# A decoder layer in fp32 pairs: tokens loaded channels-first, RMS norm moved behind the projections

## The chip, the cores and the metric

The kernel runs on one core of one Trainium2 chip. The metric is the device time of one execution in microseconds (us); the profile's clock starts at the first instruction, and its span is a little shorter than the device time.

## What is computed

One layer for 512 tokens of 1024 channels, all in fp32. Cut to what matters here:

```python
def rmsnorm(x, g):
    y = x * lax.rsqrt(jnp.mean(x * x, axis=-1, keepdims=True) + EPS)
    return y * g

h = rmsnorm(x, g_mix)
z = h @ w_in                       # 1024 -> 9728 columns
rq, rk, rv, rg, aq, ak, av, gl = jnp.split(z, IN_OFFSETS, axis=-1)
# retention on rq, rk, rv with swish gate rg: ret_branch
# QK-norm and rotary on aq, ak; three attention groups with av: att_branch
gate_r, gate_a = jnp.split(jax.nn.sigmoid(gl + b_gate), 2, axis=-1)
x = x + (gate_r * ret_branch + gate_a * att_branch) @ w_o
x = x + jnp.square(jax.nn.relu(rmsnorm(x, g_mlp) @ w_up)) @ w_down
gate_p = jax.nn.sigmoid(rmsnorm(x, g_ple) @ w_ple_gate)
return x + gate_p * (p_i @ w_ple_proj)       # p_i: 512 x 256 embeddings
```

The factor 1/rms is one number for each token, so `(x * r * g) @ w` equals `r * ((x * g) @ w)`.

## The kernel before

Every matrix is held as a pair: a high part (`whi`, `hh`), rounded to the matmul's format by ScalarE, and a low part (`wlo`, `hl`), the rest, by VectorE. A product is three matmuls (`mm3`): high by high, high by low, low by high. The weights come in units of 512 KB; `plan` lists them in order of use. `fetch` loads a unit into one of 6 buffers (`raw`), `ahead` and `split_unit` turn it into the pair (4 buffers each). A unit of `w_in` is split with the gain `g_mix` on its rows (lines 226 to 229): one instruction of 128x512 on each engine for each 128 input channels, two for a unit of rows, four of 128x256 for a unit of the gates. A unit of another weight is split in one instruction of 128x1024, or in halves of 128x512 while `self.pinned` is set.

The projections put channels on the partitions as the contraction. `rows_gemm` makes token tiles (128 tokens by 512 columns) in four PSUM banks (`pg`); a bank is used again when `consume` has taken the one before out of it. `cols_gemm` makes channel tiles by 512 tokens (gates, MLP).

The order of work on each engine is that of the program text; Tile puts in the semaphores, and nothing overtakes on an engine. Deferred work (transposes, attention scores) stands in `self.queue` and is put in by `tick`, once every two k steps or so; a lag counts ticks.

The start goes as follows. `setup` queues all loads on SyncE (SP), at most eight in flight. The embeddings `p` come with tokens on the partitions, are transposed on TensorE (`pp`) and multiplied with `w_ple_proj` (`embed`: two halves of four token tiles, stored by `store` to DRAM for the end of the kernel). `norm_T` makes a token tile's sum of squares, 1/rms (`rstd`: VectorE `v`, GpSimd `r`) and `y = x * r`, then `split_T` transposes it on TensorE (`pt`) and writes the pair `hT`. Tiles 0 and 1 are normed inside `embed`, tiles 2 and 3 inside the first projection, the queries of attention group 0, which is written as a wave (`wave=norm`): unit m and token tile m come in together. Two small transposes (`turn`) bring the gain vectors onto the partitions.

Then come, in order: queries, keys and values of group 0, the same of groups 1 and 2, retention, the gates with the two output projections (`mix`), and the tail (`w_o`, MLP, the embeddings' gate). For each token tile of a query or key projection (`att_proj`, `consume`) ScalarE copies the bank to `zn` and squares it by heads, VectorE and GpSimd make the norm (`v`, `r`), VectorE multiplies, and `rotate` applies the rotary tables `C` and `S` (GpSimd one product, VectorE two and a sum, all named `ro`). `tables` builds `C` and `S` on GpSimd out of loaded constants (`rotc`, and the gains in `mg`). Twelve ticks later `heads_T` transposes the four tiles by heads (`ph`).

Of the kernel before, what the change touches and what calls it, by code (L numbers as in the profile page):

```python
# [75 lines left out]
class Block:  # L76
# [63 lines left out]
    def evac(self, out, in_):  # L140
        self.ev ^= 1
        if self.ev:
            self.nc.scalar.activation(out, in_, AF.Copy)
        else:
            self.nc.vector.tensor_copy(out, in_)
# [256 lines left out]
    def setup(self):  # L402
        nc, a = self.nc, self.a
        rows = self.const.tile([48, P], F32, name="rows")
        names = ("g_mix", "ret_gn", "g_mlp", "g_ple", "b_gate")

        def row_loads(ns):
            for n in ns:
                o, k = 8 * names.index(n), a[n].shape[1] // P
                nc.sync.dma_start(rows[o : o + k], a[n][0].rearrange("(k p) -> k p", p=P))  # L410

        self.p_raw = self.wraw.tile([P, 1024], F32, tag="raw", name="p_raw").rearrange("p (t e) -> p t e", t=NT)
        nc.sync.dma_start(self.p_raw, a["p"][0, 0].rearrange("(t p) e -> p t e", p=P))
        self.fetch(1)
        row_loads(names[:1])
# [18 lines left out]
        self.gcol = self.const.tile([P, 48], F32, name="gcol")  # L434

        def turn(lo, hi):
            ps = self.bank()
            nc.tensor.transpose(ps[:, lo:hi], rows[lo:hi], self.ident[lo:hi, lo:hi])
            nc.vector.tensor_copy(self.gcol[:, lo:hi], ps[:, lo:hi])

        self.turn_mix = lambda: turn(0, 8)
        row_loads(names[1:])
        self.turn_rows = lambda: turn(0, 48)

# [22 lines left out]
    def embed(self, norm):  # L467
        nc = self.nc
        self.pinned = True
        pT = self.big("pT")  # L470
        hi, lo = pT[:, 0:2], pT[:, 2:4]
        for g in range(2):
            ps = self.bank("pp")
            for t in range(2):
                for k in range(2):
                    nc.tensor.transpose(ps[:, (2 * k + t) * P : (2 * k + t + 1) * P],
                                        self.p_raw[:, 2 * g + t, k * P : (k + 1) * P], self.ident)
            pv = ps.rearrange("p (k t) -> p k t", k=2)
            o = slice(2 * g * P, 2 * (g + 1) * P)
            self.pin(nc.scalar.activation(R(hi[:, :, o]), pv, AF.Copy))  # L480
            nc.vector.tensor_tensor(R(lo[:, :, o]), pv, hi[:, :, o], op=ALU.subtract)
        self.turn_mix()
        self.pp_dram = self.dram.tile([S, D], F32, name="pp_dram", tag="pp_dram")
        for half in range(2):
            def store(t, ps):
                o = self.tmp("pp")
                self.evac(o, ps)
                nc.sync.dma_start(self.pp_dram[t * P : (t + 1) * P, 512 * half : 512 * (half + 1)], o)

            self.ahead(1)  # L490
            norm(half)
            if half == 0:
                self.ahead(2)
            else:
                self.force(("h", 0, 1))
# [47 lines left out]
    def att_proj(self, g, n, **kw):  # L543
# [4 lines left out]
        def consume(t, ps):  # L548
# [3 lines left out]
            nc.scalar.activation(zn, ps, AF.Copy)  # L552
# [510 lines left out]
```

## Time and profile before

| | |
|---|---|
| median of 3 runs | 1037.51 us (1036.36 to 1038.64) |
| profiled execution | 1038.66 us |
| its span | 1036.7 us, granted clock 0.996 |
| TensorE matmul busy | 1014.2 us (98%), 4810 instructions |
| VectorE busy | 676.6 us (65%) |
| ScalarE busy | 480.4 us (46%) |
| GpSimd busy | 137.8 us (13%) |
| moved by DMA | 128.81 MB, 124 GB/s in the mean |

A matmul is shown until its result has left the array, so a 128x512 matmul shows about 0.39 us while the next one starts 0.23 us after it. How fast TensorE goes is read from the starts. In rows of the timeline an engine comes after the start and the duration; "x2" joins neighbours of one kind; brackets tell how long the engine had been idle and who ended it. In rows of stretches each engine has its busy time and number of instructions, and the DMA's share and rate stand at the end.

### The profile page before, as it was taken

What the parts mean: (1) busy time and instruction counts of PE and PEld (TensorE: products, weight loads), DVE (VectorE), ACT (ScalarE), POOL (GpSimd) and SP (SyncE); (2) the same over time, 40 slices, a digit from 0 to 9 for tenths busy, and PEclk for the clock granted to TensorE, in tenths of its full rate; (3) what the DMA queues carried; (4) which work ended last, traced back from release to release, by engine and by line L of the source; (5) the groups of instructions that cost most, each with busy time, mean ns of one, the idle gap of its engine ahead of it and who ended that gap; (6) DMA issues with size and microseconds to landing.
All of it is one profiled execution on the core that took longest, in us unless ns stands there. A gap on an engine that the chain in (4) does not pass through costs nothing.

```text
span 1036.7 us, 12913 instructions
## 1 busy us (share of the span) xinstructions
PE 1014.2 (98%) x4810; PEld 848.4 (82%) x4810; DVE 676.6 (65%) x1017; ACT 480.4 (46%) x1012; POOL 137.8 (13%) x126
## 2 busy tenths in 40 slices
PE   8998989999999999999999999999999999999998
PEld 6776878988987788888888888988888888888877
DVE  5588766767686743545343344679769877867983
ACT  6534635465452442535342323665455355355461
POOL 0264043123025501000010000000000000000000
PEclk9999999999999999999999999999999999999999
DMA  9532312323321222222323422354753753845711
GB/s 330 180 116 69 99 42 63 101 62 102 102 69 54 82 82 81 82 82 68 96 89 115 162 85 78 103 183 161 233 175 124 241 166 120 265 160 184 243 63 59
DMA packets 84766, 128.81 MB, mean 124 GB/s; under 512 B 6576, under 2 KB 39392, under 8 KB 84704
## 3 DMA queue, kind: packets, MB, share of 16 engines
q1 hardware_dynamic: 84704, 128.00, 38.7%
q8 instruction: 37, 0.61, 0.2%
q14 instruction: 25, 0.20, 0.1%
HBM read 123.77 MB, written 4.21 MB: 123 GB/s over the span
## 4 chain that ended last, share of the span: by engine, by line
PE 81%; DVE 8%; issue 2%; POOL 2%; ACT 1%; DMA 0%; DVEq 0%; ACTq 0%; POOLq 0%
PE pg L256 23%; PE pg L258 23%; PE pg L257 23%; DVE ro L510 2%; PE pb L256 2%; PE pb L258 2%; PE pb L257 2%; DVE wlo L224 1%; PE ph L522 1%; DVE wlo L229 1%; PE pt L365 1%; POOL r L355 1%; PE po L638 1%; PE sc L615 1%; DVE ro L512 1%
## 5 line engine op out<-in xcount | busy, mean ns | idle before, releaser
L256 PE MATMUL pg<-whi,hh 128*128 128x512 f32 x480 | 201.7, 421 | 1.6 <-ACT zn L552 0.8
L257 PE MATMUL pg<-wlo,hh 128*128 128x512 f32 x480 | 189.7, 395 | 2.1 <-DVE wlo L229 2.1
L258 PE MATMUL pg<-whi,hl 128*128 128x512 f32 x480 | 189.5, 395 | 0.0
L223 ACT ACTIVATE whi<-raw 128x1024 fp32r<-128x1024 f32 (+1 forms) x120 | 123.6, 1043 | 131.9 <-PE pg L257 39.0
L224 DVE TENSOR_TENSOR wlo<-raw,whi 128x1024 fp32r<-128x1024 f32 (+1 forms) x120 | 146.2, 1230 | 36.8 <-ACT whi L223 35.7
L229 DVE SCALAR_TENSOR_TENSOR wlo<-raw,gcol,whi 128x512 fp32r<-128x512 f32 (+1 forms) x184 | 122.2, 704 | 64.1 <-ACT whi L228 63.9
L228 ACT ACTIVATE whi<-raw,gcol 128x512 fp32r<-128x512 f32 (+1 forms) x184 | 107.4, 639 | 86.3 <-PE pg L258 53.1
L355 POOL TENSOR_TENSOR r<-v,mhalf 128x1 f32<-128x1 f32 (+1 forms) x52 | 40.5, 778 | 653.0 <-DVE v L354 653.0
L257 PEld LDWEIGHTS pg<-wlo,hh 128*128 128x128 f32 x480 | 99.3, 207 | 18.2 <-DVE wlo L229 4.6
L258 PEld LDWEIGHTS pg<-whi,hl 128*128 128x128 f32 x480 | 98.6, 205 | 17.4 <-DVE hl L379 0.4
L256 PEld LDWEIGHTS pg<-whi,hh 128*128 128x128 f32 x480 | 98.9, 206 | 16.2 <-ACT whi L228 1.2
L256 PE MATMUL pg<-h2h,whi 128*128 128x512 f32 (+1 forms) x288 | 105.5, 367 | 0.0
L257 PE MATMUL pg<-h2l,whi 128*128 128x512 f32 (+1 forms) x288 | 105.3, 366 | 0.0
L258 PE MATMUL pg<-h2h,wlo 128*128 128x512 f32 (+1 forms) x288 | 105.2, 366 | 0.0
L258 PEld LDWEIGHTS pg<-h2h,wlo 128*128 128x128 f32 x288 | 54.3, 189 | 8.8
L257 PEld LDWEIGHTS pg<-h2l,whi 128*128 128x128 f32 x288 | 54.3, 189 | 8.6
L256 PEld LDWEIGHTS pg<-h2h,whi 128*128 128x128 f32 x288 | 54.2, 189 | 8.7
L256 PE MATMUL pg<-hh,whi 128*128 128x512 f32 x128 | 52.4, 410 | 0.0
L257 PE MATMUL pg<-wlo,uh 128*128 128x512 f32 x128 | 50.1, 391 | 0.0
L258 PE MATMUL pg<-hh,wlo 128*128 128x512 f32 x128 | 50.0, 391 | 0.0
L257 PE MATMUL pg<-hl,whi 128*128 128x512 f32 x128 | 49.9, 390 | 0.0
L258 PE MATMUL pg<-whi,ul 128*128 128x512 f32 x128 | 49.9, 390 | 0.0
(176 smaller groups left out, 1838.4 us busy)
## 6 DMA issues: line engine op xcount, KB each, us to landing
raw<-in_w_down SPq DMA_DIRECT2D x80, 512.0 KB, 3.4
raw<-in_w_in SPq DMA_DIRECT2D x76, 512.0 KB, 3.8
raw<-in_w_up SPq DMA_DIRECT2D x32, 512.0 KB, 4.6
raw<-in_w_ret_out SPq DMA_DIRECT2D x8, 512.0 KB, 3.4
raw<-in_w_o SPq DMA_DIRECT2D x8, 512.0 KB, 3.5
raw<-in_w_ple_gate SPq DMA_DIRECT2D x8, 512.0 KB, 4.8
x<-in_x SPq DMA_DIRECT2D x8, 256.0 KB, 6.1
pp_dram<-pp SPq DMA_DIRECT2D x8, 256.0 KB, 4.1
```

The source lines that it names most:

```text
L223: self.pin(nc.scalar.activation(R(hi[:, i]), raw[:, i], AF.Copy))
L224: nc.vector.tensor_tensor(R(lo[:, i]), raw[:, i], hi[:, i], op=ALU.subtract)
L228: self.pin(nc.scalar.activation(R(hi[:, i]), raw[:, i], AF.Copy, scale=g))
L229: nc.vector.scalar_tensor_tensor(R(lo[:, i]), raw[:, i], g, hi[:, i], op0=ALU.mult, op1=ALU.subtract)
L256: t.matmul(ps, sh, mh, start=first, stop=False, skip_group_check=more)
L257: t.matmul(ps, sh, ml, start=False, stop=False, skip_group_check=more)
L258: t.matmul(ps, sl, mh, start=False, stop=last, skip_group_check=more)
L355: self.nc.gpsimd.tensor_tensor(r, v, self.mhalf[:, :w], op=ALU.pow)
L365: nc.tensor.transpose(ps[:, k * P : (k + 1) * P], part[:, k * P : (k + 1) * P], self.ident)
L510: nc.vector.tensor_tensor(v4(t2)[:, :, o0 : o0 + 64], v4(zn)[:, :, i0 : i0 + 64], bc(Sn[:, o0 : o0 + 64], 64), op=ALU.mult)
L512: nc.vector.tensor_tensor(o, t1, t2, op=ALU.add)
L522: self.nc.tensor.transpose(ps[:, t * P : (t + 1) * P], rots[t][:, h * HD : (h + 1) * HD], self.ident)
```

## The change

The host now hands over x, p and the gain vectors a second time, transposed (`x_cols`, `p_cols`, `vec_cols`); x is loaded in both forms. `embed` splits the transposed p, then multiplies x by g_mix channel by channel and splits that into `hT`, with no norm and no transpose. The first units of `w_in` are split in between, without gain. `token_factors` makes 1/rms of all 512 tokens from the other copy of x, and sends it through DRAM once to get it in the strided token order (`r_perm`). The queries of group 0 are no longer a wave. Where a projection leaves PSUM the token's factor is applied: as the scale of a copy (`zn`, `rz`, `v`), of a sigmoid, or, for the gates with tokens along the free axis, by a product with `r_free`, the factors spread over all partitions by four transposes.

```diff
-    def evac(self, out, in_):
+    def evac(self, out, in_, scale=None):
...
-            self.nc.scalar.activation(out, in_, AF.Copy)
+            self.nc.scalar.activation(out, in_, AF.Copy, **({} if scale is None else {"scale": scale}))
+        elif scale is not None:
+            self.nc.vector.tensor_scalar(out, in_, scale, None, op0=ALU.mult)
...
     def plan_rows(self, w, c0, nk, r0=0):
-            self.plan.append((w[...], 2 * u if w is self.w_in else None))
+            self.plan.append((w[...], None))
...
     def setup(self):
+        self.p_raw = self.wraw.tile([P, 1024], F32, tag="raw", name="p_raw").rearrange("p (k t) -> p k t", k=2)
+        for k in range(2):
+            nc.sync.dma_start(self.p_raw[:, k], a["p_cols"][k * P : (k + 1) * P])
+        self.fetch(2)
+        nc.sync.dma_start(self.gcol, a["vec_cols"])
+        for u in range(KD // 2):
+            v = xr[u // 2][:, 2 * (u % 2) : 2 * (u % 2) + 2]
+            nc.sync.dma_start(v, a["x_cols"][256 * u : 256 * (u + 1)].rearrange("(k p) t -> p k t", p=P))
+        self.fetch(4)
         for t in range(NT):
-            for h in range(2):
-                nc.sync.dma_start(v[:, c], a["x"][0, t * P : (t + 1) * P, c])
-            self.fetch(t + 2)
+            nc.sync.dma_start(v, a["x"][0, t * P : (t + 1) * P])
...
     def embed(self):
+        self.pinned = True
+        for k in range(2):
+            self.pin(nc.scalar.activation(R(hi[:, k]), self.p_raw[:, k], AF.Copy))
+            nc.vector.tensor_tensor(R(lo[:, k]), self.p_raw[:, k], hi[:, k], op=ALU.subtract)
+        self.ahead(2)
+        self.hT = self.new_act(2, "h")
+        for k in range(KD):
+            g = self.gcol[:, k : k + 1]
+            h, l = (part[k // 4][:, k % 4] for part in self.hT)
+            self.pin(nc.scalar.activation(R(h), self.x_cols[k], AF.Copy, scale=g))
+            nc.vector.scalar_tensor_tensor(R(l), self.x_cols[k], g, h, op0=ALU.mult, op1=ALU.subtract)
+            if k % 2:
+                self.ahead(2 + (k + 1) // 2)
+        self.pinned = False
...
+    def token_factors(self):
+        for t in range(NT):
+            nc.scalar.activation(j, self.x_tiles[t], AF.Square, accum_out=ss[:, t : t + 1])
+        nc.vector.tensor_scalar(v, ss, 1.0 / D, EPS, op0=ALU.mult, op1=ALU.add)
+        nc.gpsimd.tensor_tensor(self.r, v, self.mhalf[:, :NT], op=ALU.pow)
+        nc.sync.dma_start(d.rearrange("(t p) c -> p (t c)", p=P), self.r)
+        nc.sync.dma_start(self.r_perm, d.rearrange("(l r) c -> l (r c)", r=DIL))
+
+    def spread_factors(self):
+        for t in range(NT):
+            self.nc.tensor.transpose(ps[:, t * P : (t + 1) * P], self.r[:, t : t + 1].to_broadcast([P, P]), self.ident)
+        self.nc.scalar.activation(self.r_free, ps, AF.Copy)
...
-            nc.scalar.activation(zn, ps, AF.Copy)
+            nc.scalar.activation(zn, ps, AF.Copy, scale=self.r[:, t : t + 1])
...
-                nc.scalar.activation(s, ps, AF.Sigmoid)
-                nc.vector.tensor_tensor(G[:, t], s, ps, op=ALU.mult)
+                nc.scalar.activation(s, ps, AF.Sigmoid, scale=r)
+                nc.vector.scalar_tensor_tensor(G[:, t], ps, r, s, op0=ALU.mult, op1=ALU.mult)
...
-                        nc.scalar.activation(s, ps, AF.Sigmoid, bias=self.gcol[:, b : b + 1])
+                        nc.vector.tensor_tensor(s, ps, self.r_free, op=ALU.mult)
+                        nc.scalar.activation(s, s, AF.Sigmoid, bias=self.gcol[:, b : b + 1])
...
-        self.embed(norm)
+        self.embed()
+        self.token_factors()
         self.load_tables()
-        groups = [self.attention(g, **({"wave": norm} if g == 0 else {})) for g in range(NG)]
+        groups = [self.attention(g) for g in range(NG)]
```

Two places show how the order moves. The first is SyncE's queue of loads from the start. In the kernel before (`rows` are the gain vectors, the first `raw` of `in_w_in` is the first unit of the queries; a `x2` joins two issues):

```order
L413 DMA p_raw<-in_p 128x4x256
L189 DMA raw_87<-in_w_ple_proj 128x2x512
L410 DMA rows<-in_g_mix 8x128
L422 DMA x_90<-in_x 128x512 x2
L189 DMA raw_94<-in_w_ple_proj 128x2x512
L422 DMA x_90<-in_x 128x512 x2
L189 DMA raw_98<-in_w_in 128x2x512
L422 DMA x_91<-in_x 128x512 x2
L189 DMA raw_102<-in_w_in 128x2x512
L422 DMA x_91<-in_x 128x512 x2
L189 DMA raw_106<-in_w_in 128x2x512
```

The third unit of the queries, `raw_106`, stood behind nine times 512 KB: p, two units of `w_ple_proj`, x, two units of `w_in`. In the changed kernel the same queue begins so:

```order
L408 DMA p_raw<-in_p_cols 128x512 x2
L191 DMA raw_87<-in_w_ple_proj 128x2x512
L191 DMA raw_89<-in_w_ple_proj 128x2x512
L411 DMA gcol<-in_vec_cols 128x48
L416 DMA xr_93<-in_x_cols 128x2x512 x2
L416 DMA xr_94<-in_x_cols 128x2x512 x2
L191 DMA raw_99<-in_w_in 128x2x512
L191 DMA raw_101<-in_w_in 128x2x512
L423 DMA x_103<-in_x 128x1024 x2
L423 DMA x_104<-in_x 128x1024 x2
L191 DMA raw_168<-in_w_in 128x2x512
L191 DMA raw_180<-in_w_in 128x2x512
```

Now the third unit, `raw_168`, is behind both copies of x, 13 times 512 KB. Further on in the same queue the factors' way through DRAM stands between the loads of the constants:

```order
L479 DMA pp_dram<-pp_266 128x512
L495 DMA r_dram<-r 128x4x1
L444 DMA mg_286<-in_c_mask 128x512
L448 DMA mg_286<-in_q_gain 128x384
L450 DMA mg_286<-in_q_gain 128x3x64
L497 DMA r_perm<-r_dram 128x4
L450 DMA mg_286<-in_q_gain 128x3x64
L448 DMA mg_286<-in_k_gain 128x384
```

The second half of the turned query gain is behind the load of `r_perm`, which waits for the store of `r`; before, all loads of the gains followed the mask with no such wait.

The second place is ScalarE's queue in the changed kernel, from the first channels of x on (`hh` is the high part of `hT`, `whi_148` to `whi_182` are the query's units, `pp` empties a bank of `embed`, `j` are the squares for the token factors):

```order
L469 ACTIVATE hh_140<-xr_93,gcol 128x512 x2
L225 ACTIVATE whi_148<-raw_99 128x512 x2
L469 ACTIVATE hh_140<-xr_93,gcol 128x512 x2
L225 ACTIVATE whi_158<-raw_101 128x512 x2
L469 ACTIVATE hh_141<-xr_94,gcol 128x512 x2
L143 ACTIVATE pp_196<-pg_189 128x512
L225 ACTIVATE whi_170<-raw_168 128x512 x2
L469 ACTIVATE hh_141<-xr_94,gcol 128x512 x2
L489 ACTIVATE j_270,ss_269<-x_103 128x1024 x2
L143 ACTIVATE pp_216<-pg_209 128x512
L143 ACTIVATE pp_236<-pg_229 128x512
L489 ACTIVATE j_270,ss_269<-x_104 128x1024 x2
```

In the kernel before, the same engine had these rows there (`j` the squares of one token tile, `hh` its transposed high part):

```order
L223 ACTIVATE whi_150<-raw_87 128x512 x2
L388 ACTIVATE j_157,ss_156<-x_90 128x512
L388 ACTIVATE j_159,ss_156<-x_90 128x512
L223 ACTIVATE whi_171<-raw_94 128x512 x2
L143 ACTIVATE pp_184<-pg_177 128x512
L378 ACTIVATE hh_127<-pt_187 128x4x128
L378 ACTIVATE hh_128<-pt_204 128x4x128
L143 ACTIVATE pp_218<-pg_211 128x512
```

So the copies that free the banks of `embed` now stand behind splits of weights that belong to the projection after it. VectorE follows the same pattern: its first copy out of a bank, `pp_206`, comes right behind the low parts of `whi_170` and of the last two channels' blocks.

More of the change, by code (lines that the diff above doesn't have):

```diff
@@ L403, in setup @@
         nc, a = self.nc, self.a
[L404 to L415, printed above, removed]
+        self.p_raw = self.wraw.tile([P, 1024], F32, tag="raw", name="p_raw").rearrange("p (k t) -> p k t", k=2)
+        for k in range(2):
+            nc.sync.dma_start(self.p_raw[:, k], a["p_cols"][k * P : (k + 1) * P])
+        self.fetch(2)
+        self.gcol = self.const.tile([P, 48], F32, name="gcol")
+        nc.sync.dma_start(self.gcol, a["vec_cols"])
+        xr = [self.big("xr") for _ in range(2)]
+        self.x_cols = []
+        for u in range(KD // 2):
+            v = xr[u // 2][:, 2 * (u % 2) : 2 * (u % 2) + 2]
+            nc.sync.dma_start(v, a["x_cols"][256 * u : 256 * (u + 1)].rearrange("(k p) t -> p k t", p=P))
+            self.x_cols += [v[:, 0], v[:, 1]]
+        self.fetch(4)
         self.x_tiles = []
@@ L433, in setup @@
         nc.gpsimd.memset(self.mhalf, -0.5)
[L434 to L443, printed above, removed]
     def load_tables(self):
@@ L464, in load_tables, with embed @@
         self.gains = gv
-    def embed(self, norm):
+    def embed(self):
         nc = self.nc
-        self.pinned = True
         pT = self.big("pT")
         hi, lo = pT[:, 0:2], pT[:, 2:4]
[L472 to L482, printed above, removed]
+        self.pinned = True
[12 more added lines that the diff above has]
+        self.pinned = False
         self.pp_dram = self.dram.tile([S, D], F32, name="pp_dram", tag="pp_dram")
@@ L488, in store @@
                 nc.sync.dma_start(self.pp_dram[t * P : (t + 1) * P, 512 * half : 512 * (half + 1)], o)
[L490 to L495, printed above, removed]
-            self.rows_gemm(([hi], [lo]), 2, store)
-        self.force(("h", 1, 1))
-        self.pinned = False
+            self.rows_gemm(([hi], [lo]), 2, store)
+    def token_factors(self):
+        nc = self.nc
+        ss = self.small(NT, "ss")
+        for t in range(NT):
+            j = self.big("j").rearrange("p a b -> p (a b)")[:, :D] if t == 0 else j
+            nc.scalar.activation(j, self.x_tiles[t], AF.Square, accum_out=ss[:, t : t + 1])
+        v = self.small(NT, "v")
+        self.r = self.const.tile([P, NT], F32, name="r")
+        nc.vector.tensor_scalar(v, ss, 1.0 / D, EPS, op0=ALU.mult, op1=ALU.add)
+        nc.gpsimd.tensor_tensor(self.r, v, self.mhalf[:, :NT], op=ALU.pow)
+        d = self.dram.tile([S, 1], F32, name="r_dram", tag="r_dram")
+        nc.sync.dma_start(d.rearrange("(t p) c -> p (t c)", p=P), self.r)
+        self.r_perm = self.const.tile([P, NT], F32, name="r_perm")
+        nc.sync.dma_start(self.r_perm, d.rearrange("(l r) c -> l (r c)", r=DIL))
+    def spread_factors(self):
+        ps = self.bank("pc")
+        for t in range(NT):
+            self.nc.tensor.transpose(ps[:, t * P : (t + 1) * P], self.r[:, t : t + 1].to_broadcast([P, P]), self.ident)
+        self.r_free = self.tabp.tile([P, S], F32, tag="tab", name="r_free")
+        self.nc.scalar.activation(self.r_free, ps, AF.Copy)
     def rotate(self, zn, C, Sn):
@@ L1052 @@
     data.update(shape_constants())
+    data["x_cols"] = np.ascontiguousarray(inputs["x"][0].T)
+    data["p_cols"] = np.ascontiguousarray(inputs["p"][0, 0].T)
+    data["vec_cols"] = np.ascontiguousarray(np.concatenate(
+        [inputs[n][0] for n in ("g_mix", "ret_gn", "g_mlp", "g_ple", "b_gate")]).reshape(-1, P).T)
     arrays, aps = {}, {}
```

19 lines of the change are left out of this document (8 added, 11 removed).

## The prediction

> **What bounds the kernel now.** I read the page first, then the busy times by stretch, then TensorE's timeline at the start, and last the waits around 50 to 100 us.
>
> ```profile
> PE 1014.2 (98%) x4810; PEld 848.4 (82%) x4810; DVE 676.6 (65%) x1017; ACT 480.4 (46%) x1012; POOL 137.8 (13%) x126
> ...
> 2.00:4.00 2.00, 1.34 (x4) 0.16 (x2) 0.00 (x0) 0.01 (x1) 0.00 (x0) 1.00 0.81 238
> 4.00:14.00 10.00, 8.10 (x31) 5.95 (x32) 6.03 (x13) 5.91 (x13) 0.55 (x1) 1.00 1.06 389
> 14.00:24.00 10.00, 9.95 (x47) 7.66 (x46) 5.76 (x12) 6.46 (x14) 0.56 (x1) 1.00 1.05 357
> 49.00:98.00 49.00, 42.99 (x191) 33.26 (x191) 40.57 (x57) 22.08 (x73) 26.47 (x20) 1.00 0.29 86
> 98.00:153.00 55.00, 51.72 (x276) 43.91 (x275) 41.52 (x66) 27.97 (x89) 13.73 (x11) 0.98 0.26 78
> 328.00:346.00 18.00, 14.70 (x70) 11.35 (x69) 14.35 (x19) 6.04 (x10) 12.95 (x11) 0.91 0.05 8
> ```
>
> After the stretch come busy PE, PEld, DVE, ACT, POOL, the granted clock, the DMA's share and GB/s. TensorE bounds the kernel as a whole. Three places differ. Up to 24 us the DMA is full (share 1.05) and the data's arrival sets the pace. From 49 to 98 us VectorE is busy 40.57 of 49 us, and TensorE idles 6.0. In 98 to 153 and 328 to 346 us TensorE idles 3.3 each. A change at the start counts only by what is left of it behind 98 us, where TensorE is the bound again.
>
> ```profile
> 4.90 1.94 PE L476 MATMUL pp<-ident,p_raw 128*128 128x128 f32 x8 [1.56 <-DMA p_raw<-in_p]
> ...
> 8.04 1.22 PE L256 MATMUL pg<-whi,pT 128*128 128x512 f32 x2 [1.00 <-ACT whi L223]
> ...
> 10.11 0.63 PE L256 MATMUL pg<-whi,pT 128*128 128x512 f32 x1
> 10.53 0.63 PE L257 MATMUL pg<-wlo,pT 128*128 128x512 f32 x1
> ...
> 31.39 1.03 PE L365 MATMUL pt<-ident,y 128*128 128x128 f32 x8
> ...
> 49.04 0.39 PE L256 MATMUL pg<-whi,hh 128*128 128x512 f32 x1
> 49.27 0.39 PE L257 MATMUL pg<-wlo,hh 128*128 128x512 f32 x1
> ...
> 66.83 0.49 PE L522 MATMUL ph<-ident,ro 128*128 128x128 f32 x3
> 69.15 0.33 PE L522 MATMUL ph<-ident,ro 128*128 128x128 f32 x1 [1.83 <-DVE ro L512]
> ...
> 95.51 0.49 PE L522 MATMUL ph<-ident,ro 128*128 128x128 f32 x3
> 97.61 0.33 PE L522 MATMUL ph<-ident,ro 128*128 128x128 f32 x1 [1.62 <-DVE ro L512]
> ```
>
> 49.04 is the first matmul of group 0's keys; matmuls then start 0.227 us apart. At 10.11 they start 0.42 apart: about half rate, and the granted clock still says 1.00. Full rate came near 11.5, some 3.4 us after 8.04. At 69.15 and 97.61 the transposes of queries and keys wait for VectorE's last rotary sum: those are the ends of a chain on VectorE and GpSimd, and 97.61 is my checkpoint.
>
> **The change part by part.** Durations for the steps:
>
> ```profile
> L224 DVE TENSOR_TENSOR wlo<-raw,whi 128x1024 fp32r<-128x1024 f32 x116 | 143.6, 1249 | 36.8 <-ACT whi L223 35.7 <-PE ry L802 0.4
> L223 ACT ACTIVATE whi<-raw 128x1024 fp32r<-128x1024 f32 x116 | 121.3, 1058 | 131.9 <-PE pg L257 39.0 <-PE pg L258 28.6 <-DVE raw L205 26.1
> L229 DVE SCALAR_TENSOR_TENSOR wlo<-raw,gcol,whi 128x512 fp32r<-128x512 f32 x120 | 93.7, 815 | 31.5 <-ACT whi L228 31.3
> L228 ACT ACTIVATE whi<-raw,gcol 128x512 fp32r<-128x512 f32 x120 | 79.3, 714 | 65.4 <-PE pg L258 52.8 <-issue 8.7 <-DMA raw<-in_w_in 3.7
> L388 ACT ACTIVATE j<-x 128x512 f32<-128x512 f32 x24 | 14.9, 625 | 7.4 <-DVE x L947 7.4
> L145 DVE COPY pp<-pg 128x512 f32<-128x512 f32 x4 | 2.7, 687 | 2.1 <-PE pg L258 2.1
> L224 DVE TENSOR_TENSOR wlo<-raw,whi 128x512 fp32r<-128x512 f32 x4 | 2.6, 684 | 0.0
> L143 ACT ACTIVATE pp<-pg 128x512 f32<-128x512 f32 x4 | 2.4, 598 | 3.4 <-PE pg L258 3.4
> L223 ACT ACTIVATE whi<-raw 128x512 fp32r<-128x512 f32 x4 | 2.3, 619 | 0.0
> ```
>
> *Removed from TensorE:* 40 transposes of p and y, two of gain vectors, at 0.11 to 0.13 us (1.03 us for eight): about 5 us, all before 62 us, where data and VectorE set the pace. I book nothing for them by themselves; the start is worked out anew.
>
> *The start.* By 4 us 0.48 MB were moved, then 0.389 MB/us; p's 0.52 MB were through at 4.1, and its user started at 4.90, so a load is usable 0.8 us after its last byte. In the new order the first query unit is complete after 4.22 MB (p 0.52, `w_ple_proj` 1.05, gains 0.02, x by channels 2.10, the unit 0.52), at 13.6 + 0.8 = 14.4 us; the second at 15.8; the third, `whi_170`'s, behind 2.10 MB of x by tokens, after 7.36 MB, at 21.7 + 0.8 = 22.5 (23.2 by the 357 of 14 to 24 us, which has stores in it; loads alone, I take 22.5).
>
> The Trainium skill, page "DMA: Bandwidth & Descriptors", section "Specifications", gives about 358 GB/s as HBM's limit for a core. By it the third unit would come at 24.0; the stretch of 10 us at 389 disagrees, and the measurement decides.
>
> ScalarE, in its order: unit one 14.4 to 15.6 (2 x 0.62), two blocks of hT to 17.1 (2 x 0.71), unit two to 18.3, two blocks to 19.7, `pp_196` to 20.3. Then it waits for unit three, 22.5 to 23.7; two blocks to 25.2; squares of x at about 1.1 for 1024 (an estimate between twice 0.625 and the 1.058 of a copy) to 27.4; `pp_216` to 28.0. VectorE is one low part behind the blocks, 25.9, and copies `pp_206` to 26.7 (0.69).
>
> TensorE: `embed` starts near 6.8 (the first `w_ple_proj` unit: 1.05 MB is through at 5.5, usable at 6.3, plus 0.6), a good 1 us earlier than 8.04, fills four banks by about 13.8 and stands until 20.4 for `pp_196`; six matmuls; stands until 26.8 for `pp_206`; 18 more. At full rate these take 4.1 us and the queries start at 30.9. The only rows here on matmuls after a pause show half rate for 3.4 us: 8 matmuls in 3.4, ten in 2.3, start at 32.5. Both pauses (6 and 4 us) are longer than any later one in this trace, so I take half rate, and keep both. The queries, 96 x 0.227 = 21.8, end at 52.7 or 54.3: the keys start 3.7 or 5.3 us later than at 49.04.
>
> *How the chain takes this up.*
>
> ```profile
> 41.10 0.60 ACT L552 ACTIVATE zn<-pg 128x512 f32<-128x512 f32 x1 [0.78 <-ACT hh L378]
> 43.04 0.17 DVE L354 TENSOR_SCALAR v<-ss 128x4 f32<-128x4 f32 x1 [1.65 <-ACT j L556]
> ...
> 59.00 0.15 DVE L354 TENSOR_SCALAR v<-ss 128x4 f32<-128x4 f32 x1
> 61.10 1.47 POOL L507 TENSOR_TENSOR ro<-zn,C 128x512 f32<-128x512 f32 x1 [0.86 <-issue]
> 63.56 0.16 DVE L354 TENSOR_SCALAR v<-ss 128x4 f32<-128x4 f32 x1
> ...
> 67.10 1.45 POOL L536 TENSOR_TENSOR C<-rotc,mg 128x512 f32<-128x512 f32 x1
> ...
> 71.91 1.73 POOL L536 TENSOR_TENSOR S<-rotc,mg 128x512 f32<-128x512 f32 x1
> ...
> 76.05 0.69 DVE L558 TENSOR_TENSOR zn<-zn,r 128x512 f32<-128x512 f32 x1 [1.12 <-POOL r L355]
> ```
>
> A tile needs 1.9 us from `zn` to `v` and the chain 4.6 a tile (59.00 to 63.56). With half rate the first tile's bank is full at 32.5 + 60 x 0.227 = 46.1, `v` at 48.3; two tiles to 57.5, two low parts of weights (2 x 1.25) to 60.0, the fourth tile's `v` at 64.6, its end at 69.2. TensorE wants the transposes at 54.3 + 72 x 0.227 = 70.6: the wait of 1.83 at 69.15 is gone. GpSimd ends the fourth tile's product 3.6 us behind its `v` (59.00 to 62.57), at 68.2, makes four tables as now (67.10 to near 73.6) to 74.7, then the keys' `r` of 1.0: their first `zn` at 75.8, against 76.05. The 5.3 us are swallowed: before, the queries' tiles were early and waited for VectorE. From there to the checkpoint before took 21.56 us. Four half units (4 x 0.815 = 3.26) become two whole ones (2.50) in it: 96.6 against 97.61, -1.0. TensorE itself is there in time: keys end at 54.3 + 21.8 + 1.8 = 77.9, 72 matmuls to 94.2, about 2 us of waits for the second half of the values' weights, as the 6.0 idle has now. With the full rate the same sum gives -2.6.
>
> *Behind the checkpoint.* 32 more units lose 2 x 0.815 - 1.25 = 0.38 each on VectorE. TensorE can gain from none (0) to all of its idle (6.6). The nearest row is 49 to 98, where a block of four tiles gains 0.8; two such blocks would make 1.5, and since the tables and waits for GpSimd stay and a scaled `zn` costs 0.1 more a tile (0.714 against 0.619), I book -0.5. The gates' 16 extra products (0.68) and the sigmoid behind lie beside 5 us of matmuls each; their cover is TensorE's work on the next bank, and without it they would cost 0.7 apiece. ScalarE's saving hides nothing: it is not on the path. The four transposes for `r_free` cost 0.5 where TensorE has no idle. Values scaled on VectorE replace copies of the same size.
>
> Sum: -1.0 - 0.5 + 0.5 = -1.0 against the profiled execution of 1038.66 (span 1036.7, and 2.0 around it), which itself is 1.15 above the median. Against the median 1037.51: 1036.5. What can be told from no change is 0.2%, 2.1 us.
>
> **The rivals.**
>
> *The clock stays up.* Then -2.6 at the checkpoint: 1034.9. For it: nothing in the trace shows a pause of this length. Against: the half rate at 10.11 came after a patchy start.
>
> The Trainium skill, page "TensorE: Matmul & The Clock Gate", section "Why this matters for your kernels", speaks against this rival: pauses of more than about 3 us between bursts bring the half rate back. By that rule my forecast holds; the trace agrees at 10.11 and has no later pause to test it.
>
> *VectorE's relief counts in full.* Half of the 6.6 idle comes back: 1036.5 - 3.3 + 0.5 = 1033.7. For it: VectorE is busy 41.52 of 55 there. Against: the chain's waits are for GpSimd.
>
> *Slower: the tables come late.* `C` and `S` of the queries stand on GpSimd ahead of the first tile's `r`, and the last load of their gain is now behind the round trip of `r`.
>
> ```profile
> mg<-in_q_gain SPq DMA_DIRECT2D x2, 96.0 KB, 7.5
> ...
> mg<-in_k_gain SPq DMA_DIRECT2D x2, 96.0 KB, 10.5
> ...
> st0p<-st_dram SPq DMA_DIRECT2D x1, 16.0 KB, 4.6
> ```
>
> `r` goes out near 34, comes through at 38.6 (4.6 as the nearest small transfer), the gain is issued at 39.1 and lands between 43.7 (4.6) and 49.6 (10.5). Two tables (1.5 + 1.7) end at 46.9 or 52.8; `r` of the first tile wants GpSimd at 48.5. I take 43.7, since loads ahead have drained by then, whereas the 7.5 and 10.5 were taken behind a full DMA. At 10.5 the whole chain slips by 4.3: 1040.8. It decides from a landing later than 48.4 on, 9.3 us after the issue.
>
> **How the numbers follow.** My forecast (1036.5, own range 1035 to 1038.5) gets 0.50: a fifth of it lies below 1035.4. The clock 0.15, two thirds faster; the relief 0.15, nearly all faster; the late tables 0.15, four fifths slower; 0.05 for what I don't see. Faster 0.10 + 0.10 + 0.14 + 0.02 = 0.36; slower 0.12 + 0.02 + 0.03 = 0.17; same 0.47. The range 1032.5 to 1040.5 takes in the relief and most of the late tables.
>
> **What would show it.** TensorE idle around 14 to 20 and 21 to 27 us, ended by `pp` copies; half rate from 27 on; keys starting near 54; no wait at the queries' transposes; the keys' first `zn` near 76; the transposes of the keys released near 96.6. I am wrong if the keys' `zn` comes beyond 79 (tables, or loads slower than 389), or if idle behind 98 us changes by more than 2 us.

## The result and the profile after

| | before | changed |
|---|---|---|
| first job, median (range) | 1037.29 us (1036.36 to 1038.64) | 1044.56 us (1040.62 to 1045.36) |
| ratio, 95% interval | | 1.0057 (1.0035 to 1.0078) |
| profiled execution, its span | 1038.66, 1036.7 | 1040.62, 1038.9 |
| granted clock in it | 0.996 | 0.993 |
| VectorE, ScalarE busy | 676.6, 480.4 us | 664.1, 460.5 us |

The change makes the kernel slower by about 6 us by the ratio (the medians differ by 7.3). The prediction said 1036.5, with 1040.5 as the upper end. The changed kernel's runs lie apart, and that is part of the answer: two at 1040.6 and 1041.2 with granted clocks of 0.993 and 0.991, three at 1044.6 to 1045.4 with 0.987 to 0.990. The profile is of the shortest, so it shows only the first part of the loss. One run each of two kernels below (`e1_again` at 2304.94 us, `e9_before_cover` at 1265.10 us) was in a slow state and is left out of their medians and ratios.

The description ahead of the prediction says that the order on an engine is that of the program text. That isn't so throughout: unless an instruction is pinned, Tile's scheduler can move it. Below, two instructions of ScalarE change places in a kernel (`e8_before_whole`) whose only edit is the way the weights are split. One of the losses comes from that.

TensorE's timeline of the changed kernel, the rows with the longest waits (start, duration, and in brackets how long it had stood and for whom):

```profile
7.63 1.22 PE L258 MATMUL pg<-whi,pT 128*128 128x512 f32 x2 [4.29 <-ACT whi L225]
20.43 0.79 PE L258 MATMUL pg<-whi,pT 128*128 128x512 f32 x1 [4.53 <-ACT pp L143]
21.02 0.63 PE L259 MATMUL pg<-wlo,pT 128*128 128x512 f32 x1
21.45 0.63 PE L260 MATMUL pg<-whi,pT 128*128 128x512 f32 x1
27.10 0.80 PE L258 MATMUL pg<-whi,pT 128*128 128x512 f32 x1 [3.74 <-DVE pp L147]
32.72 0.39 PE L258 MATMUL pg<-whi,hh 128*128 128x512 f32 x1
98.41 0.33 PE L528 MATMUL ph<-ident,ro 128*128 128x128 f32 x1 [1.59 <-DVE ro L518]
152.08 1.29 PE L643 MATMUL po<-pT,v 128*128 128x128 f32 x8 [4.38 <-DVE pT L147]
343.27 0.66 PE L528 MATMUL ph<-ident,ro 128*128 128x128 f32 x4 [3.33 <-DVE mt L705]
```

The start ends as forecast: pauses until 20.43 and 27.10 (20.4 and 26.8 were said), matmuls 0.43 apart behind them, which is half rate, queries from 32.72 (32.5). Only the first pause is shorter, 4.53 us where 6 were said, since `embed` began at 7.63 instead of 6.8 and filled its banks later. The wait at the queries' transposes is gone. But the checkpoint, the release of the keys' transposes, is at 98.41 and not at 96.6. In the kernel before, the waits that end at 152.08 and 343.27 here were shorter:

```profile
150.44 1.32 PE L638 MATMUL po<-pT,v 128*128 128x128 f32 x8 [2.07 <-DVE pT L145]
341.25 0.66 PE L522 MATMUL ph<-ident,ro 128*128 128x128 f32 x4 [1.99 <-DVE mt L700]
```

So the lead of the kernel before is 0.8 us at the checkpoint, 1.6 at 152 and 2.0 at 343. It stays there: the spans differ by 2.2. The other 4 us, between this run and the median, go with a lower granted clock (0.987 to 0.990 against 0.993); the long runs have no trace. The same stretches of both kernels (busy times of PE, PEld, DVE, ACT, POOL, then the granted clock), the kernel before first:

```profile
16.00:32.00 16.00, 15.95 (x77) 12.64 (x76) 9.45 (x19) 8.25 (x18) 1.11 (x2) 1.00 0.85 262
148.00:160.00 12.00, 9.93 (x43) 8.15 (x42) 4.18 (x6) 3.23 (x5) 2.91 (x2) 0.86 0.00 0
340.00:352.00 12.00, 10.76 (x45) 8.83 (x46) 10.84 (x13) 4.43 (x7) 8.73 (x6) 0.86 0.16 45
```

```profile
16.00:32.00 16.00, 7.83 (x21) 5.80 (x22) 9.75 (x16) 12.56 (x23) 0.69 (x1) 0.79 1.05 388
148.00:160.00 12.00, 7.92 (x32) 6.62 (x33) 3.92 (x4) 1.64 (x2) 4.41 (x3) 0.86 0.00 0
340.00:352.00 12.00, 8.73 (x36) 7.17 (x37) 8.51 (x11) 4.00 (x6) 11.12 (x7) 0.86 0.30 87
```

Both lose clock behind the two later waits. Only the changed kernel loses it at the start too.

### The profile page after: what moved, and what is told of

Read it like the earlier page. It is cut to its first block, busy times and chain, and to the rows that moved or that the text cites. A ratio compares the mean times of both kernels' runs of the same rounds, so it can differ in the third digit from the quotient of the medians.

```text
span 1038.9 us, 12633 instructions
## 1 busy us (share of the span) xinstructions
PE 1009.2 (97%) x4772; PEld 847.0 (82%) x4772; DVE 664.1 (64%) x912; ACT 460.5 (44%) x901; POOL 142.0 (14%) x123
## 4 chain that ended last, share of the span: by engine, by line
PE 85%; DVE 7%; issue 2%; DMA 2%; POOL 2%; ACT 1%; SPq 0%; ACTq 0%; DVEq 0%; POOLq 0%
PE pg L258 25%; PE pg L260 25%; PE pg L259 25%; DVE wlo L226 2%; PE pb L260 2%; PE pb L259 2%; PE pb L258 2%; DVE ro L516 1%; PE ph L528 1%; DMA raw<-in_w_in 1%; PE pt L367 1%; POOL r L357 1%; DMA xr<-in_x_cols 1%; PE po L643 1%; PE sc L620 1%
## 5 line engine op out<-in xcount | busy, mean ns | idle before, releaser
L226 DVE TENSOR_TENSOR wlo<-raw,whi 128x1024 fp32r<-128x1024 f32 (+1 forms) x200 | 246.2, 1244 | 97.5 <-ACT whi L225 95.9
L225 ACT ACTIVATE whi<-raw 128x1024 fp32r<-128x1024 f32 (+1 forms) x200 | 203.7, 1031 | 232.9 <-PE pg L260 101.3
L259 PE MATMUL pg<-wlo,hh 128*128 128x512 f32 x480 | 189.2, 394 | 1.1 <-DVE wlo L226 1.1
L357 POOL TENSOR_TENSOR r<-v,mhalf 128x4 f32<-128x4 f32 (+1 forms) x48 | 38.3, 798 | 609.7 <-DVE v L356 609.5
L258 PE MATMUL pg<-whi,uh 128*128 128x512 f32 x128 | 49.9, 390 | 0.0
L207 DVE TENSOR_TENSOR raw<-raw,raw 128x1024 f32<-128x1024 f32 x32 | 39.0, 1220 | 12.2 <-DMA raw<-in_w_down 12.2
```

What stands on the lines that cost most here:

```text
L207: self.nc.vector.tensor_tensor(raw, raw, g0, op=ALU.add)
L225: self.pin(nc.scalar.activation(R(hi[:, i]), raw[:, i], AF.Copy))
L226: nc.vector.tensor_tensor(R(lo[:, i]), raw[:, i], hi[:, i], op=ALU.subtract)
L258: t.matmul(ps, sh, mh, start=first, stop=False, skip_group_check=more)
L259: t.matmul(ps, sh, ml, start=False, stop=False, skip_group_check=more)
L357: self.nc.gpsimd.tensor_tensor(r, v, self.mhalf[:, :w], op=ALU.pow)
```

## The experiments

Two theories stood against each other. Theory 1: the clock, brought down by TensorE's pauses. Theory 2: the chain of short instructions on VectorE and GpSimd, which whole weight units and late tables disturb. Twelve kernels ran, four to a job, each job on one chip with its own runs of the kernel before. Two kernels are set against each other directly only within a job; between jobs it goes by the ratios (0.1% is 1.04 us).

| | median | before in the job | ratio (95%) |
|---|---|---|---|
| `e1_again` | 1043.12 | 1038.37 | 1.0052 (1.0037 to 1.0068) |
| `e2_fill` | 1041.17 | 1038.37 | 1.0028 (1.0016 to 1.0041) |
| `e3_xlate` | 1041.34 | 1038.37 | 1.0034 (1.0021 to 1.0047) |
| `e4_halves` | 1043.37 | 1038.37 | 1.0049 (1.0034 to 1.0064) |
| `e5_gains` | 1040.36 | 1037.01 | 1.0032 (1.0019 to 1.0044) |
| `e6_cover3` | 1038.60 | 1037.01 | 1.0015 (1.0006 to 1.0024) |
| `e7_order` | 1039.75 | 1037.01 | 1.0026 (1.0015 to 1.0038) |
| `e8_before_whole` | 1038.64 | 1037.01 | 1.0016 (1.0007 to 1.0025) |
| `e9_before_cover` | 1035.05 | 1036.61 | 0.9983 (0.9974 to 0.9992) |
| `e10_all` | 1032.91 | 1036.61 | 0.9961 (0.9946 to 0.9975) |
| `e11_all_halves` | 1032.88 | 1036.61 | 0.9960 (0.9947 to 0.9974) |
| `e12_all_nocover` | 1037.81 | 1036.61 | 1.0004 (0.9993 to 1.0014) |

**The changed kernel again** (no edit).

> The changed kernel once more, to see how its times spread and where TensorE's granted clock goes. The first runs of it took 1040.6, 1041.2 and 1044.6 to 1045.4, with mean granted clocks of 0.993, 0.991 and 0.987 to 0.990; the profile is of the shortest. Theory 1 (clock): the extra 4 us of the long runs are stretches at a reduced granted clock, set off by TensorE's pauses (16 to 20 and 21 to 27 us, 149 to 152, 340 to 343); runs again at about 1041 and 1045, longer runs with the lower clock. Theory 2 (the chain on VectorE and GpSimd): one time of 1040 to 1042 with the 2.2 us of span that the traces show, and the scatter has nothing to do with the clock.

1042.26 to 1043.96; the shortest, at a clock of 0.992, is the profiled one, the others have 0.987 to 0.989. Longer goes with the lower clock, as theory 1 says, but the two groups of the first job are not seen: the other four are at 1042.9 to 1044.0.

**Matmuls in the two pauses at the start.** Their results are not used; they only keep TensorE at work ("cover" from here on).

```diff
-            self.rows_gemm(([hi], [lo]), 2, store)
+            def cover(t):
+                if half == 1 and t < 2:
+                    ps = self.bank("fill")
+                    for _ in range((20, 22)[t]):
+                        self.tc.keep_in_program_order(
+                            nc.tensor.matmul(ps, R(hi[:, 0, :P]), R(hi[:, 0]), start=True, stop=True))
+            self.rows_gemm(([hi], [lo]), 2, store, need=cover)
```

> 20 and 22 matmuls on data already there, into a bank of their own that nobody reads, stand in TensorE's two pauses at the start; nothing else differs. Theory 1: the clock stays granted, the queries start at 31 instead of 32.7, there is no run at 1045, and the median falls to 1040 or below. Theory 2: the queries start at 31, but the queries' tables still come at 49 and the keys' transposes are released at 98.4, so that the time is that of the changed kernel's shorter runs, 1040 to 1041, and long runs are as frequent as before.

2.0 us less than the changed kernel in the same job, no run above 1042.4, clocks of 0.994 to 0.997. So the start's clock is worth some 2 us, and without its loss the longest runs don't occur. Theory 2's part stays: the rest is still 2.9 us slower than before, and the two later waits are what they were:

```profile
97.04 0.33 PE L535 MATMUL ph<-ident,ro 128*128 128x128 f32 x1 [1.57 <-DVE ro L525]
150.71 2.08 PE L650 MATMUL po<-pT,v 128*128 128x128 f32 x8 [4.39 <-DVE pT L147]
342.83 0.66 PE L535 MATMUL ph<-ident,ro 128*128 128x128 f32 x4 [3.36 <-DVE mt L712]
```

**The third unit ahead of x by tokens.**

```diff
-        self.fetch(4)
+        self.fetch(6)
```

> The third unit of the queries is loaded ahead of the copy of x with tokens on the partitions instead of behind it, and the fourth still behind. Theory 1: TensorE's second pause shrinks from 3.7 to at most 1 us, and with it the half rate; keys start near 52 instead of 54.5, and the time is 1038 to 1041. Theory 2: 1/rms of the tokens comes no earlier, so the first tile's r stays near 49 and the release of the keys' transposes near 98: 1040 to 1041. If both hold, the median falls by the long runs alone.

TensorE's second wait fell from 3.74 to 0.90 us and the queries started at 30.66. The first tile then stood ready and waited for its tables, as GpSimd and then VectorE of this run show:

```profile
47.83 1.29 POOL L542 TENSOR_TENSOR S<-rotc,mg 128x512 f32<-128x512 f32 x1 [2.32 <-DMA mg<-in_q_gain]
49.08 1.02 POOL L357 TENSOR_TENSOR r<-v,mhalf 128x4 f32<-128x4 f32 x1
```

```profile
46.56 0.17 DVE L356 TENSOR_SCALAR v<-ss 128x4 f32<-128x4 f32 x1 [2.49 <-ACT j L562]
50.13 0.69 DVE L564 TENSOR_TENSOR zn<-zn,r 128x512 f32<-128x512 f32 x1 [3.40 <-POOL r L357]
```

`v` was there at 46.56, `r` began at 49.08: the tables' 2.4 us. The keys' transposes came at 98.36, as in the changed kernel's profile. The median fell by 1.8 us all the same: the runs are at 1040.8 to 1042.8, where the changed kernel's were at 1042.3 to 1044.0 in this job, with clocks of 0.991 to 0.992 instead of 0.987 to 0.992. Each theory is right on its own part.

**Units of rows in halves.**

```diff
-            for i in range(k) if self.pinned else [slice(0, k)]:
+            for i in range(k) if self.pinned or (k == 2 and len(self.loaded) < 62) else [slice(0, k)]:
```

> The rows' units of w_in are split in two pieces of 128x512 on each engine as in the kernel before, but without gain; all the rest is the changed kernel. Theory 2 (the whole units of 1.2 us stand in the way of the chain's short instructions on VectorE, and slow GpSimd beside them): the keys' transposes are released near 97.5 instead of 98.4, the wait near 150 falls from 4.4 to about 2 us, and the time falls by 1.5 to 3 us, to 1038 to 1039. Theory 1 (clock): the wait may move, but the start and its clock stay, so the time stays at 1041 to 1045. The prediction's own step (whole units relieve VectorE): 1 us slower than the changed kernel.

A miss for theory 2: 1043.37 against 1043.12. The wait near 150 fell to 3.67, the one near 342 stayed at 3.35, and the keys' transposes came at 98.72. From there to the values near 150 the trace has 53.0 us instead of 53.7, but the size of the pieces alone gives nothing back in time.

**The tables' gains ahead of the factors' way through DRAM**, on top of `e3_xlate`.

```diff
+    def turn_factors(self):   # store of r to r_dram and load of r_perm, moved out of embed's end
...
         self.load_tables()
+        self.turn_factors()
```

> As in the run with the third unit ahead of x by tokens, and besides the factors' way through DRAM (store and strided load of r) is issued behind the loads of the constants instead of ahead of them, so that q_gain no longer stands behind it on SyncE. Theory 2 (the chain): there the first tile's v was ready at 46.6 and waited for the tables until 49.1; with the tables by 45 its r starts at 46.8, the second tile's v comes about 2.3 earlier (51.1), the keys' transposes are released at 96.1 instead of 98.4, the wait near 150 at 149.7, and the median falls from 1041.3 to about 1039. Theory 1 (clock): the start and the pauses are the same, so the clock stays 0.992 and the time 1041.

The tables were done at 44.0, and the first `r` waited for its own data:

```profile
42.73 1.29 POOL L545 TENSOR_TENSOR S<-rotc,mg 128x512 f32<-128x512 f32 x1 [1.48 <-DMA mg<-in_q_gain]
48.10 1.02 POOL L357 TENSOR_TENSOR r<-v,mhalf 128x4 f32<-128x4 f32 x1 [4.08 <-DVE v L356]
```

TensorE began 1.03 us later in this run (8.66 against 7.63), and the keys' transposes came at 97.36: 88.7 us behind that beginning against 90.7 without the edit. The chain gained its 2 us. The time did not show it (1.0032 against 1.0034): its clock was 0.989 or 0.990 in all runs, against 0.991 to 0.992, and in the profile the way from the values near 151 to the transposes near 343 took 192.5 us against 191.2, with a granted clock of 0.66 instead of 0.83 between 150 and 160. So 1.3 of the 2 us went to the clock there.

**Cover in all four pauses**, on top of `e2_fill`.

```diff
             po = self.bank("po")
+            if g == 0 and r == NT - 1:
+                for _ in range(16):
+                    self.tc.keep_in_program_order(
+                        nc.tensor.matmul(po, R(self.hT[0][0][:, 0, :P]), R(self.hT[0][0][:, 0]), start=True, stop=True))
...
         def head(h):
+            if lag == 7 and h == 2 and not self.covered:
+                self.covered = True
+                for _ in range(13):
+                    self.tc.keep_in_program_order(
+                        self.nc.tensor.matmul(self.cur, R(self.zero), R(self.hT[0][0][:, 0]), start=False, stop=False))
             ps = self.bank("ph")
```

> As in the run with matmuls in the two pauses at the start, and besides 16 matmuls into the bank of the last attention values of group 0 ahead of its own, and 13 with a zero operand (they add nothing) ahead of the third transposes of the retention's queries, where TensorE stood 4.4 and 3.4 us. Theory 1: the clock is granted all through (0.998 to 1.0), TensorE no longer runs at half rate behind 150 and 342, and the median falls from 1041.2 to about 1039. Theory 2: the pauses themselves are the loss; covering them changes nothing, 1041.

`self.cur` is the accumulation that is open at that place. It came as theory 1 had it: the granted clock is full in the three stretches, and the time 1038.6.

```profile
16.00:32.00 16.00, 15.98 (x71) 12.76 (x70) 9.98 (x17) 12.97 (x25) 0.69 (x1) 1.00 1.05 389
148.00:160.00 12.00, 11.22 (x58) 9.45 (x57) 5.31 (x5) 2.72 (x3) 3.56 (x3) 1.00 0.03 3
340.00:352.00 12.00, 11.02 (x53) 8.43 (x52) 9.56 (x12) 4.84 (x6) 9.57 (x6) 1.00 0.31 89
```

Of the 5.4 us (ratio 1.0052) 1.6 are left.

**One copy of ScalarE back to its place**, on top of `e2_fill`. ScalarE's rows around 337 us, of the kernel before and of the changed kernel:

```profile
334.83 0.60 ACT L722 ACTIVATE rz<-pg 128x512 f32<-128x512 f32 x1 [5.86 <-DVE ro L512]
337.14 1.15 ACT L709 ACTIVATE oh<-mt 128x512 fp32r<-128x512 f32 x1 [1.71 <-POOL mt L705]
```

```profile
337.82 1.13 ACT L714 ACTIVATE oh<-mt 128x512 fp32r<-128x512 f32 x1 [8.05 <-POOL mt L710]
338.74 0.65 ACT L727 ACTIVATE rz<-pg,r 128x512 f32<-128x512 f32 x1
```

Before, the copy `rz` of the third tile stood ahead of `oh`; now it stands behind, ScalarE waits 8 us for GpSimd, and everything from `rz` on comes late.

```diff
+                    ins = nc.scalar.activation(R(nat(oh[:, h])), av, AF.Copy)
+                    if h == 2:        # written behind the next rz, and pinned there
+                        self.tc.keep_in_program_order(ins)
```

> As in the run with matmuls in the two pauses at the start, and one instruction of ScalarE moved: the copy rz of the third token tile of the retention's keys goes ahead of the third head's oh, as it did in the kernel before. Theory 2 (order): the wait of the retention's transposes falls from 3.4 to about 2.0 us (before: 1.99) and the median from 1041.2 to 1039.5 or 1040; if the granted clock behind it is then better too, down to 1039. Theory 1 (start clock alone): no change, 1041.2. If another link of the chain ends the wait, the pause stays above 3 us.

`rz` is back at 334.95, and the wait is that of the kernel before:

```profile
341.36 0.66 PE L537 MATMUL ph<-ident,ro 128*128 128x128 f32 x4 [1.97 <-DVE mt L714]
```

So the order makes the 1.4 us of this wait. The median is 1039.75, as expected by theory 2, but in another job than `e2_fill`; that the 1.4 us reach the time is not shown: 1.0026 against 1.0028.

**The kernel before with whole units** (the gain is left out of `w_in`).

```diff
-            self.plan.append((w[...], 2 * u if w is self.w_in else None))
+            self.plan.append((w[...], None))
```

The same is done in `plan_cols`, for the gates' units.

> The kernel before with the gain left out of the units of w_in (the output lacks g_mix), so that these units are split whole, 128x1024 in one instruction on each engine, as in the changed kernel; x is normed and transposed as before. It does this one part of the change alone. The prediction's step (whole units relieve VectorE: -0.8 a block of four tiles, -1.5 to -2 in all): 1036 to 1037. Theory 2 (whole units stand ahead of short instructions of the chain and slow GpSimd beside them): the wait near 150 starts or ends about 0.8 us later, the ScalarE order at the retention may turn as it did in the changed kernel, and the time is 1038.4 to 1041. Theory 1 (clock): same time as before, 1038.4, unless a pause grows beyond 3 us.

It is 1.6 us slower than the kernel before, and the part of the change that was to bring the gain does this by itself. TensorE, then ScalarE, then the stretch that the prediction took its gain from:

```profile
97.53 0.33 PE L522 MATMUL ph<-ident,ro 128*128 128x128 f32 x1 [1.53 <-DVE ro L512]
151.03 2.08 PE L638 MATMUL po<-pT,v 128*128 128x128 f32 x8 [3.30 <-DVE pT L145]
342.20 1.12 PE L522 MATMUL ph<-ident,ro 128*128 128x128 f32 x4 [3.34 <-DVE mt L700]
```

```profile
336.73 1.14 ACT L709 ACTIVATE oh<-mt 128x512 fp32r<-128x512 f32 x1 [8.15 <-POOL mt L705]
337.66 0.63 ACT L722 ACTIVATE rz<-pg 128x512 f32<-128x512 f32 x1
```

```profile
49.00:98.00 49.00, 43.49 (x196) 34.25 (x196) 40.47 (x50) 20.95 (x66) 30.05 (x21) 1.00 0.28 86
```

The checkpoint moves by 0.1, not 0.8; both later waits grow; `rz` falls behind `oh` here too. VectorE is busy 40.47 us between 49 and 98, where it was 40.57: fewer instructions, no less time.

**The kernel before with cover** (8 and 8 matmuls, same edit as above in the two later places).

> The kernel before, with 8 matmuls into the bank of the last attention values of group 0 and 8 with a zero operand ahead of the third transposes of the retention's queries, where it stood 2.1 and 2.0 us. Theory 1 (clock): the granted clock is 0.999 or 1.0 instead of 0.996 to 0.998, and the time is 1 to 1.5 us below the kernel before, as its own runs at 1.0 are (1035.2 to 1036.5 against 1037 to 1038.4). So at the full clock the changed kernel (1038.6 with its pauses covered) is still 2.5 us behind: that part is the order. If the time is that of the kernel before, the clock's price in it is nothing, and the 4.8 us between the changed kernel and its covered version are more than the clock.

Its clock is 0.998 to 1.0, and the time 1.6 us less by the medians, 1.8 by the ratio:

```profile
148.00:160.00 12.00, 11.90 (x61) 9.99 (x60) 4.97 (x6) 3.62 (x6) 2.73 (x2) 1.00 0.08 18
340.00:352.00 12.00, 11.79 (x60) 9.59 (x59) 10.82 (x13) 5.59 (x9) 9.03 (x7) 1.00 0.20 52
```

At the full clock the changed kernel is thus 1.0015 less 0.9983, 0.32% or 3.3 us, behind the one before; with their own clocks it was 5.4. The clock costs the one 1.8 us, the other 3.8. These are ratios from different jobs, each with an interval of 0.9 to 1.6 us to either side.

**All that helped, together**: `e3_xlate`, `e5_gains`, the order of `e7_order`, and cover (20, 3, 16 and 8 matmuls).

> The changed kernel with all that helped: third unit ahead of x by tokens, tables' gains ahead of the factors' round trip, rz ahead of the third oh, and TensorE covered in the pauses (20 and 3 matmuls at the start, 16 and 8 later). The whole units stay. Theory 1 and 2 add up: from 1038.6 (covered) take 1.4 (order) and 1 to 2 (tables early): 1035.2 to 1036.2, at a clock of 1.0; that is 1 to 2 us below the kernel before and level with its covered version. If the wait near 150 is fixed by something else than the tables, 1037.

**The same with halves.**

> As the run with all of it, and the rows' units of w_in split in halves of 128x512 again (13 matmuls in the wait near 150 instead of 16). Theory 2: the stretch from the release of the keys' transposes to the values near 150 takes 53.0 instead of 53.65 us, as it did with halves alone, and the time is 0.6 us shorter, 1034.6 to 1035.6. If VectorE's work counts by its sum, halves cost 0.12 us each more and it is 0.5 to 1 us longer.

**The same with halves, without cover.**

> As the run with all of it and halves, but no matmul is put into any pause. It differs by the clock alone. Theory 1: the pauses at the start (5.2 and 0.9 us) and near 150 and 341 bring the clock down to about 0.991, and the time is 3 to 4 us longer than with cover, 1038 to 1039. Theory 2 (pauses themselves): the same time as with cover, 1035 to 1036.

1032.91, 1032.88 and 1037.81. The first is 2.3 us below the expected range: 3.7 below the kernel before, and 2.1 below its covered version from the same job. The early loads gave more than was expected: in `e10_all` the checkpoint comes 86.3 us behind TensorE's first matmul of `embed`, in `e6_cover3` 89.6. Halves make no difference to the time again, though the way from the keys' transposes to the values is 0.7 us shorter with them (53.0 against 53.7). Cover is worth 4.9 us here, where theory 1 had 3 to 4. Without it the repaired kernel is only level with the kernel before (1.0004). These are the halves without cover, then with it:

```profile
16.00:32.00 16.00, 10.46 (x31) 7.85 (x32) 10.93 (x18) 13.95 (x26) 1.03 (x1) 0.68 1.05 390
148.00:160.00 12.00, 10.70 (x40) 9.01 (x41) 3.30 (x6) 2.90 (x5) 1.77 (x2) 0.72 0.00 0
340.00:352.00 12.00, 10.83 (x53) 8.86 (x54) 10.82 (x14) 5.14 (x9) 8.69 (x6) 1.00 0.14 44
```

```profile
16.00:32.00 16.00, 13.82 (x60) 10.80 (x59) 11.70 (x19) 14.22 (x26) 1.03 (x1) 1.00 1.05 391
148.00:160.00 12.00, 12.00 (x58) 10.04 (x59) 2.75 (x5) 4.88 (x14) 0.78 (x2) 1.00 0.25 79
340.00:352.00 12.00, 11.91 (x59) 9.66 (x58) 10.90 (x13) 5.54 (x9) 8.46 (x6) 1.00 0.36 99
```

In these two profiles the spans are 1035.4 and 1031.4. The covered one reaches the checkpoint 1.9 us earlier after TensorE's first matmul of `embed` (86.5 against 88.4, with the queries from 29.2 instead of 30.6), and from the values near 150 to the transposes near 341 it takes 189.2 us against 191.8. The way from checkpoint to values is 53.0 in both, so the covered waits end for the same reason at the same distance. What differs is the rate behind the pauses: the clock.

## Why the prediction was wrong

The forecast was 1.0 us less than before. The repeat `e1_again` has 5.4 more (1.0052): 3.3 of them stay at the full clock, and about 2 are the clock.

*The start* was right, as quoted: half rate, queries at 32.7. So was the swallowing of most of the queries' delay up to the fourth tile: its `v` came at 64.88 (64.6 was said; 63.56 before).

*The failed step: "four half units become two whole ones, 96.6 against 97.61, -1.0".* The checkpoint went to 98.41. Two parts of the sum failed. "Four tables as now" took 7.6 us, not 6.5. These are GpSimd and VectorE of the changed kernel, and below them VectorE of the one before:

```profile
68.43 1.47 POOL L542 TENSOR_TENSOR C<-rotc,mg 128x512 f32<-128x512 f32 x1
69.86 1.73 POOL L542 TENSOR_TENSOR S<-rotc,mg 128x512 f32<-128x512 f32 x1
71.55 2.27 POOL L542 TENSOR_TENSOR C<-rotc,mg 128x512 f32<-128x512 f32 x1
73.78 2.27 POOL L542 TENSOR_TENSOR S<-rotc,mg 128x512 f32<-128x512 f32 x1
```

```profile
70.38 4.53 DVE L226 TENSOR_TENSOR wlo<-raw,whi 128x1024 fp32r<-128x1024 f32 x2
74.83 1.26 DVE L356 TENSOR_SCALAR v<-ss 128x4 f32<-128x4 f32 x1
```

```profile
69.02 5.83 DVE L229 SCALAR_TENSOR_TENSOR wlo<-raw,gcol,whi 128x512 fp32r<-128x512 f32 x4
```

Beside a table a whole low part took 2.27 and so did the table; a half took 1.78 and the table 1.73, and the last of the four halves ran alone. I had priced the low parts at 0.815 and 1.25, their means over the kernel, and the tables as if they didn't depend on VectorE's pieces. VectorE saved 1.3 here, GpSimd lost 1.1, and the chain goes through GpSimd. The Trainium skill, page "SBUF — State Buffer", section "SBUF: two separate sides", says that a VectorE instruction with two SBUF inputs and one of GpSimd that reads SBUF take turns, each for a whole instruction. The equal 2.27 and 2.27 agree. With halves in the changed kernel (`e4_halves`) the tables took 6.6 again, but VectorE needed 5.78 for its low parts:

```profile
70.39 5.78 DVE L226 TENSOR_TENSOR wlo<-raw,whi 128x512 fp32r<-128x512 f32 x4
```

The keys' first `r` then waited for VectorE and began at 76.33, with whole units at 76.16: what one engine saves, the other loses. The other part is the keys' own tiles: from the first `zn` the checkpoint took 21.2 us, where the prediction had 20.8. From the fourth tile's `v` to the checkpoint it took 33.5 us, before 34.05. So 0.5 was gained there, where the sum had 2, and the 1.3 by which the fourth tile was late came through but for that: 0.8.

*"Behind the checkpoint: -0.5"* had the wrong sign. VectorE's busy time between 98 and 153 fell (41.52 to 40.94), but a whole unit now stands ahead of the third tile's `v`, where a half used to stand behind it. VectorE of the changed kernel, then of the one before:

```profile
138.61 1.22 DVE L226 TENSOR_TENSOR wlo<-raw,whi 128x1024 fp32r<-128x1024 f32 x1
139.75 0.16 DVE L356 TENSOR_SCALAR v<-ss 128x4 f32<-128x4 f32 x1
```

```profile
138.05 0.16 DVE L354 TENSOR_SCALAR v<-ss 128x4 f32<-128x4 f32 x1
138.46 0.75 DVE L229 SCALAR_TENSOR_TENSOR wlo<-raw,gcol,whi 128x512 fp32r<-128x512 f32 x1 [0.24 <-ACT whi L228]
```

From the checkpoint to the values near 150 it took 53.7 us instead of 52.8: that is the 0.8 us at 152. In `e8_before_whole` it took 53.5, by another row: the third tile's `v` has no whole unit ahead of it there, but a copy `oT` at 144.28 came ahead of the fourth tile's `v`, behind which it stood before. The order of `rz` and `oh` adds 1.3 to the wait at 343; 0.4 of it is left in the lead there, since the wait at 335 shrank from 0.98 to 0.52 us and one of 0.33 at 330 is gone. `e8_before_whole` has this order too, without the rest of the change. The relief's rival (1033.7) rested on the same step and falls with it.

*The late tables* were a rival, priced at 4.3 us, and came true by 0.6: S ended at 49.0, and the first `r` began at 49.13 instead of 48.5. The store of `r` to DRAM took 9.5 us from issue to landing, not the 4.6 of another transfer. `e3_xlate` and `e5_gains` show them as the next bound once the start is faster.

*The clock*, the second step that failed, was weighed at the start only. The prediction's own rows had 0.98 and 0.91 in the two later stretches. No step asked what it does to the two waits that were already there, or to the scatter between runs: 2 us more than in the kernel before, by `e6_cover3` and `e9_before_cover`.

Still open: why the clock of one kernel differs from run to run (0.987 to 0.993), which gives the 4 us between the profile and the median of the first job; and where some 1 us of the 3.3 goes that the trace of the covered kernels shows behind 341 (half of it is where the four `r_free` transposes stand).

## What to carry to other kernels

Where a chain of short instructions sets the pace, a cheaper bulk instruction on its engine can cost time: what counts is which one stands ahead of a link, and how long. Price work beside a busy neighbour by rows from beside that neighbour, not by the kernel's mean. And look at each pause of TensorE twice, once for itself and once for the clock behind it; matmuls put into the pauses bought 1.6 us in the kernel before and 4.9 in the best one, as much as all the repairs of loads and order together (1.0052 to 1.0004).

## What was not expected of the hardware

Pauses near 2 us already cost clock: the kernel before shows 0.86 behind waits of 2.07 and 1.99 us, and 1.00 with these covered. The Trainium skill, page "TensorE: Matmul & The Clock Gate", section "Why this matters for your kernels", speaks of gaps of more than about 3 us; the measurement decides. The length alone does not decide either: the run without cover waited 1.97 us at 341 and kept 1.00 behind it, as its row above shows.
